# Four pairs of conv gate tiles by seven quarter products in a Hymba-style layer on one Trainium2 core

## The chip, the core and the metric

The kernel runs on one core of a Trainium2 chip. The metric is the device time of one execution in microseconds (us). The core has a matrix engine (TensorE; PE in the profile, PEld for its weight loads), a vector engine (VectorE, DVE), a scalar engine (ScalarE, ACT), GpSimd (POOL), and queues of transfers (DMA) that are issued by SyncE (SP), GpSimd and ScalarE. TensorE writes to PSUM, the other engines work on SBUF and, GpSimd excepted in this kernel, on PSUM.

## The reference

One decoder layer over 1024 tokens of width 1024, all in float32. `w_in` has 5 x 1024 columns; each block of 1024 columns is eight tiles of 128 channels.

```
h = rmsnorm(x, norm_g) * (1.0 + scale) + shift
u = h @ w_in
cv, cg, cs, lx, ls = split(u, 5)
v = cv * sigmoid(cg)
v = causal_depthwise_conv(v, dw_w, dw_b)          # 31 taps
v = silu(layernorm(v, cln_g, cln_b))
y_conv = (v @ pw2_w + pw2_b) * silu(cs)
xs = causal_depthwise_conv(lx, sc_w, sc_b)        # 4 taps
r, i = sigmoid(blockdiag(xs, wr) + br), sigmoid(blockdiag(xs, wi) + bi)
a = exp(-8 * r * softplus(-lam)); bx = sqrt(1 - a*a) * (i * xs)
y_lru = linear_scan(a, bx) * silu(ls)
x = x + (1.0 + gate) * (concat([y_conv, y_lru]) @ w_out)
return rmsnorm(x, final_g)
```

`shift`, `scale` and `gate` come from `silu(c) @ mod_w + mod_b`.

## The kernel before

**Layout.** Channels lie on the 128 partitions, tokens along the free axis (T = 1024, in two halves of H = 512). A product of a tile of 128 output channels is taken in three matmuls for each of the eight input tiles k and each half: the weights are split into a rounded part `whi` and a rest `wlo`, the inputs into `uh` and `ul`, and whi*uh + whi*ul + wlo*uh is summed in PSUM (`mm_k`, L471). A tile is thus 8 x 2 x 3 = 48 matmuls of 128x128 weights against 512 columns. Each weight tile (512 KB) comes by one transfer into one of two `raw` buffers; ScalarE casts it to `whi` (two buffers), VectorE subtracts for `wlo` (two buffers; GpSimd for those whose number is below EARLY = 10).

**Tiles by name.** CV, CG, CS, LX and LS are the tiles of the five blocks of `w_in`. Four of them (FIRST) run while x and the modulation still arrive, three (NEXT: LS 0, CS 0, CS 1) right after, on the not yet normalised input, and are mended afterwards. Then come the other 33 in the order of `slots`, with the block-diagonal gates of an LRU tile between them; then eight LRU tiles of the out projection (`("lru", m)`, inputs `yh`, `yl`), whose results are parked in DRAM; then `pw2`; then the rest of the out projection.

**Seven quarter products.** `pw2` and three pairs of the out projection already use a Strassen-like form (Winograd's) for two output tiles at a time: `pair_weights` forms sums of the quarters of the weights (rows of even and odd k tiles by the two output tiles), `quarters` forms sums of the quarters of the operands (halves of the tokens by even and odd k tiles), and `pair_products` (L593) does seven products of 4 x 3 matmuls each, 84 in place of 96. ScalarE and VectorE join the partial sums (`e`). The names of the operands' quarters are B11 (even tile, first half), B12, B21, B22 (odd tile) and T1 to T4.

**Depthwise conv.** The 31 taps of a conv tile (`conv_tile`) are done in three chains over the even tokens, the odd ones and their sum, each on 512 elements. For five of the eight tiles the chains are 15 + 15 + 14 = 44 VectorE steps (`cacc`, `caccs`) into an accumulator in PSUM, and three half-width folds. For the tiles in POOLED (1, 3, 5) ScalarE makes each product (`cq`, `co`), and GpSimd issues transfers that add it in SBUF to `es` and `oo` (L348, `ADD`): 29 of them for a tile; VectorE does the last three folds. `conv_sum` adds the eight tiles into `csum`, six times on GpSimd and once on VectorE; `layer_norm` starts with its mean on TensorE (L1162).

**LRU.** `gates(i)` runs the two block-diagonal products of tile i, then i*xs on VectorE, `a` and the root on ScalarE, the scan and the product with silu(ls) on VectorE; `split` then makes `yh`, `yl`. **Dots.** The modulation's dot products (`dot`) multiply a tile `modw` with silu(c) and sum along the row, in one VectorE instruction each.

**Order of the work.** No loop fixes the order of the instructions. Each operation is entered in a plan (`S.op`) with an engine, a cost, a priority, and what it reads and writes. `order` (class `Plan`) then goes through simulated time, takes for each free engine the ready operation of lowest priority value that finds its buffers free, and writes the instructions out in that order; on the chip each engine runs its list in that order and waits where something isn't ready. The plan has 47 buffers of 512 KB in SBUF ("big") and three double tiles and two single ones in PSUM. It holds that a VectorE and a GpSimd operation on SBUF exclude each other (`lock`). The priority of an operation of slot n is near n; transfers have values ahead of the work that needs them.

## Time and profile before

| | us |
|---|---|
| median of 3 executions | 742.85 (742.84 to 742.89) |
| the profiled execution, its own time | 742.67 |
| its span, first to last instruction | 740.8 |
| TensorE busy | 728.4 |
| VectorE busy | 633.3 |
| ScalarE busy | 440.6 |
| GpSimd busy | 113.4 |

One execution is profiled; the 1.87 us between its own time and its span lie ahead of the first and behind the last instruction. A row of a view by groups names line, engine, operation, the tile written and the tiles read, the count, the busy time and mean duration in ns of one, and, behind a second bar, the idle time of that engine just before such an instruction with what ended it. A row of the chain of waits or of the timeline begins with its start and its length in us. A row of waits gives the sum, the count and the longest. L343 is the line of a helper through which all elementwise operations with two tensors go, so those are told apart by the names of their tiles.

### The profile page before, as it was taken

Reading aid. Unit: us, or ns where it says so; the run is one execution under the profiler, and the core shown is the slowest. Engines: PE = TensorE matmul, PEld = TensorE weight load, DVE = VectorE, ACT = ScalarE, POOL = GpSimd, SP = SyncE. Lnnn points to the kernel's source line nnn. Section 1 sums busy time; section 2 is a strip of 40 time slices with the busy share of each in tenths; the row PEclk is TensorE's granted clock in tenths of the full one; section 3 lists DMA queues with packets and bytes.
Section 4 is the critical chain, followed back from the end, with each engine's and each line's share of the span. In section 5 each row is a group of like instructions: output and inputs, shape, how many; then the busy total and the mean of one; then the engine's idle time right before and its main releaser. Section 6 shows DMA issues by size and latency. Waiting matters only on the chain.

```text
span 740.8 us, 8887 instructions
## 1 busy us (share of the span) xinstructions
PE 728.4 (98%) x3302; PEld 604.3 (82%) x3302; DVE 633.3 (85%) x847; ACT 440.6 (59%) x544; POOL 113.4 (15%) x115
## 2 busy tenths in 40 slices
PE   9999999999999999999999999999999999999995
PEld 8888887887888888888887888878888888877885
DVE  6999999899999893788499997958799767999845
ACT  7560598558858957846939777634754224455421
POOL 0033021120322233232216110010000000000003
PEclk9999999999999999999999999999999999999997
DMA  9953036673897899999573455425233430623206
GB/s 330 405 177 114 0 98 130 141 145 91 157 217 187 204 231 232 210 240 214 113 156 71 113 113 169 141 87 199 86 113 123 163 113 1 227 88 111 85 1 228
DMA packets 37340, 111.59 MB, mean 151 GB/s; under 512 B 4144, under 2 KB 12848, under 8 KB 37296
## 3 DMA queue, kind: packets, MB, share of 16 engines
q1 hardware_dynamic: 24048, 76.10, 29.2%
q0 software_dynamic: 12528, 34.26, 25.7%
q10 hardware_dynamic: 720, 0.66, 0.3%
q8 instruction: 26, 0.43, 0.2%
q14 instruction: 18, 0.15, 0.1%
HBM read 64.16 MB, written 12.58 MB: 104 GB/s over the span
## 4 chain that ended last, share of the span: by engine, by line
PE 90%; DVE 7%; ACT 2%; issue 1%; POOL 0%; DVEq 0%; POOLq 0%
PE ps L471 65%; PE papw L593 5%; PE first L735 5%; PE pbpw L593 4%; PE pbout L593 2%; PE paout L593 2%; PE gate L1126 2%; PE out L654 1%; DVE fin L335 1%; PE late L735 1%; DVE rawout L343 1%; DVE l34out L343 1%; DVE o L335 1%; DVE yu L343 0%; DVE yt L343 0%
## 5 line engine op out<-in xcount | busy, mean ns | idle before, releaser
L471 PE MATMUL ps<-uh,whi 128*128 128x512 f32 x576 | 177.9, 390 | 0.9 <-ACT sls L324 0.6
L471 PE MATMUL ps<-uh,wlo 128*128 128x512 f32 x576 | 177.4, 389 | 0.0
L471 PE MATMUL ps<-ul,whi 128*128 128x512 f32 x576 | 177.3, 389 | 0.0
L471 PEld LDWEIGHTS ps<-uh,whi 128*128 128x128 f32 x576 | 107.8, 188 | 24.7 <-ACT sls L324 1.5
L471 PEld LDWEIGHTS ps<-uh,wlo 128*128 128x128 f32 x576 | 108.1, 188 | 22.5
L471 PEld LDWEIGHTS ps<-ul,whi 128*128 128x128 f32 x576 | 108.1, 188 | 22.5
L316 ACT CAST whi<-raw 128x1024 fp32r<-128x1024 f32 x46 | 48.1, 1051 | 70.6 <-PE ps L471 59.0
L343 DVE TENSOR_TENSOR wlo<-raw,whi 128x1024 fp32r<-128x1024 f32 x40 | 50.6, 1264 | 16.3 <-ACT whi L316 16.3
L348 POOL DMA_DIRECT2D es<-cq x45 | 39.8, 900 | 134.4 <-ACT cq L324 103.0
L324 ACT ACT_TABLE_LOAD x46 | 59.0, 1283 | 1.5 <-PEq L1428 0.7
L335 DVE SCALAR_TENSOR_TENSOR cacc<-v,V,cacc 128x511 f32<-128x511 f32 (+14 forms) x75 | 55.5, 740 | 0.4
L348 POOL DMA_DIRECT2D oo<-co x42 | 38.8, 968 | 96.5 <-ACT co L324 76.9
L335 DVE SCALAR_TENSOR_TENSOR caccs<-v,V,caccs 128x511 f32<-128x511 f32 (+6 forms) x70 | 52.0, 743 | 1.0
L335 DVE SCALAR_TENSOR_TENSOR caccs<-c,wsum,caccs 128x511 f32<-128x511 f32 (+6 forms) x70 | 52.0, 742 | 0.7
L343 POOL TENSOR_TENSOR o<-fin,bc 128x256 f32<-128x256 f32 (+1 forms) x7 | 6.6, 967 | 245.5 <-ACT bc L316 245.5
L471 PE MATMUL ps<-yh,whi 128*128 128x512 f32 x128 | 40.0, 394 | 0.0
L471 PE MATMUL ps<-yh,wlo 128*128 128x512 f32 x128 | 39.4, 389 | 0.0
L471 PE MATMUL ps<-yl,whi 128*128 128x512 f32 x128 | 39.4, 389 | 0.0
L324 ACT ACTIVATE cq<-v,V 128x511 f32<-128x511 f32 (+14 forms) x45 | 31.6, 706 | 0.0
L335 DVE SCALAR_TENSOR_TENSOR xs<-ps,V,xs 128x1023 f32<-128x1023 f32 (+2 forms) x24 | 30.6, 1275 | 0.4 <-ACT xs L324 0.4
L324 ACT ACTIVATE cq<-c,wsum 128x512 f32<-128x512 f32 x42 | 29.7, 711 | 0.0
L324 ACT ACTIVATE co<-v,V 128x511 f32<-128x511 f32 (+13 forms) x42 | 29.1, 706 | 0.0
(325 smaller groups left out, 1432.5 us busy)
## 6 DMA issues: line engine op xcount, KB each, us to landing
raw<-in_w_in_dram SPq DMA_DIRECT2D x36, 512.0 KB, 4.8
modw<-in_mod_w_dram SPq DMA_DIRECT2D x24, 512.0 KB, 6.3
raw<-in_w_out_dram SPq DMA_DIRECT2D x10, 512.0 KB, 3.9
scsd<-scs SPq DMA_DIRECT2D x8, 512.0 KB, 3.4
acc<-in_xT_dram SPq DMA_DIRECT2D x8, 512.0 KB, 5.4
accd<-acc SPq DMA_DIRECT2D x8, 512.0 KB, 2.8
rawpw<-in_pw_dram SPq DMA_DIRECT2D x8, 512.0 KB, 3.5
scsr<-scsd SPq DMA_DIRECT2D x8, 512.0 KB, 5.3
```

The lines of the kernel that those rows point to most:

```text
L316: act.copy(out(), in_())
L324: act.activation(out=out(), in_=in_(), func=func, **kw)
L335: dve.scalar_tensor_tensor(out=out(), in0=in0(), scalar=scalar, in1=in1(), op0=op0, op1=op1, accum_out=accum)
L343: lambda: e.tensor_tensor(out=out(), in0=a(), in1=b(), op=op), prio, r, w,
L348: return S.op("POOL", ISSUE, lambda: pool.dma_start(out(), a(), accum_op=ALU.add), prio, r, w, lag=RATE * n / T, after=after)
L471: pe.matmul(ps()[:, a - off:b - off], k3(lhs)()[:, k, :], rhs[k]()[:, a:b], start=(k == 0 and lhs is wh and rhs is xh and (a - off) % H == 0),
L593: pe.matmul(half(*ps)(), half(*lhs)()[:, j * P:j * P + P], half(*rhs)(), start=start and j == 0 and z == 0, stop=j == KT // 2 - 1 and z == ...
L654: pe.matmul(ps()[:, a - off:e - off], k3(lhs)()[:, k, :], rhs()[:, i * H + a % H:i * H + a % H + e - a], start=k == KORD[0] and lhs is wh ...
L735: pe.matmul(ps()[:, a - off:b - off], fw_part(lhs, k, i * P, i * P + P)(), rhs()[:, a:b], start=k == 0 and lhs is wh and rhs is xh, stop=k ...
L1126: pe.matmul(ps()[:, c0:c1], lhs()[:, j, :], rhs()[:, c0:c1], start=st == 0, stop=st == 2)
```

## The change

The eight CS tiles are no longer run singly. They become four pairs (PAIRS) of seven quarter products each, behind all other tiles of `w_in` and ahead of the LRU tiles of the out projection, in the order p1, p0, p2, p3.

- Their weights come ordered by even and odd output columns, and `pair_weights` forms their sums, for pairs 0, 2 and 3 on GpSimd and for pair 1 on VectorE (WPAIR).
- The operand sums T1 to T4 of the normalised input are formed early (`h_sums`, four calls t0 to t3 in ORDER) from x, which is put into DRAM after the inputs are made and read back; differences are taken on VectorE, casts on ScalarE, rests on VectorE; the 16 results go to DRAM and come back, by transfers that GpSimd issues, when the pairs are near (`products_of_h`). B11, B21 and B22 are the inputs themselves; the buffers of the even tiles are split in two (`Split`) so that one half can be freed alone.
- `evac_pair` joins the partial sums, takes the SiLU and parks the two tiles in DRAM, as was done with each CS tile before.
- POOLED goes from three conv tiles to two (0 and 3). These keep two accumulators in turn for each chain, and GpSimd does their folds and the last adds.
- `csum` starts as a copy of one tile by a transfer and is added to by six accumulating transfers and one VectorE operation.
- The two gate products of an LRU tile (GTT) and the dots of the gate modulation (GDOT) go from VectorE to GpSimd, the latter with a sum on ScalarE.
- NEXT becomes CG 2, CV 2 and CG 3. The order of all other tiles and gates is written out (ORDER).
- Tiles that wait long (v of three conv tiles, four c, seven y, scan results) are put into DRAM and read back (`spill`, `recall`), with transfers on SP.
- Priorities, reserves and the queues of some last stores are set anew.

The core of the diff:

```diff
-NEXT = (("in", LS), ("in", CS), ("in", CS + 1))
+NEXT = (("in", CG + 2), ("in", CV + 2), ("in", CG + 3))
+PAIRS = tuple((CS + i, CS + i + 1) for i in range(0, KT, 2))
+ORDER = "i24 g0 i25 i33 g1 i32 i3 i26 g2 i35 i34 i12 i4 i36 i27 g3 i28 g4 i37 i13 t0 t1 i5 i29 g5 i30 i38 i39 i31 t2 g7 g6 i14 i6 t3 i15 i7 T p1 p0 p2 p3"
+WPAIR = ('POOL', 'DVE', 'POOL', 'POOL', 'POOL', 'POOL', 'DVE', 'POOL')
+CUTF, TFP = (5, 22)
+TSTEP, TPR = (-30.2, -34.3)
+TENG = ("DVE",) * 4
+FPLAIN = False
+VAWAY = (0, 1, 2, 4, 5)
+VP = 5
+QF = (36.4, 5.4, 32.9, 19.4, 3.9, 13.4, 28.4, 17.4)
+QL = (19.0, 10.0, 17.5, 0.5, 3.0, 22.5, 6.5, 4.0)
+CUT = 3
+HSAWAY = (0, 1, 2, 3, 4, 5, 6)
+HSR = -156.0
-SPARE = 5
+SPARE = 7
-HRES = 4
-POOLED = (1, 3, 5)
+HRES = 2
+POOLED = (0, 3)
-AP = {0: (), 512: (5,), 768: (1, 3, 5, 7)}
+AP = {0: (), 512: (1, 3, 5, 7), 768: (1, 3, 5, 7)}
-SUMS = (0, 1, 3, 2, 6, 4, 7, 5)
+SUMS = (2, 0, 1, 4, 3, 5, 6, 7)
-SPP = 30
+SPP = 25
+CSP, CBP = (-5, 20)
+AWAY = (0, 3, 6, 7)
+YAWAY = (0, 1, 2, 3, 4, 5, 7)
+YOP = 0
+XRT, XSL = "DVE", "DVE"
+GTT = 'POOL'
+WN = 3
+XSP = 6
-GDOT = "DVE"
-FOLD = "DVE"
+GDOT = 'POOL'
+FOLD = 'POOL'
-GM = 22
+GM = 19
...
     slots = list(FIRST + NEXT)
...
+    for x in ORDER.split():
+        i = int(x[1:] or 0)
+        slots.append(("in", i) if x[0] == "i" else ("gate", i) if x[0] == "g" else
+                     ("sums", 0) if x[0] == "T" else ("sums_of", i) if x[0] == "t" else
+                     ("pair", *PAIRS[i]))
     slots += [("lru", m) for m in range(KT)]
-    wslots = [s for s in slots if s[0] != "gate"] + [("out", m) for m in (4, 5, 6, 7)]
-    number = {s: n for n, s in enumerate(wslots)}
+    number = {}
+    for s in slots + [("out", m) for m in (4, 5, 6, 7)]:
+        if s[0] not in ("gate", "sums", "sums_of"):
+            number[s] = sum(1 + (z[0] == "pair") for z in number)
     B0, C0, D0 = 40, 48, 56
 
...
-    def pair_weights(kind, p, n, after, later=(), eng="DVE"):
-        src = [(w_out if kind == "out" else pw2)[2 * p + i] for i in (0, 1)]
-        name = f"{kind}{p}"
+    def pair_weights(kind, p, n, after, later=(), eng="DVE", qf=1.4, ql=2.5):
+        if kind == "in":
+            src = [w_in[m] for m in p]
+            name = f"in{p[0]}"
+        else:
+            src = [(w_out if kind == "out" else pw2)[2 * p + i] for i in (0, 1)]
+            name = f"{kind}{p}"
...
-            DMA(n - 2.5, lambda b=b: b().rearrange("p (k c) -> p k c", k=KT),
+            DMA(n - ql, lambda b=b: b().rearrange("p (k c) -> p k c", k=KT),
                 lambda i=i: src[i][:, :, :], FULL_BYTES, w=[b], after=after)
...
-        q = n - 1.4
+        q = n - qf
...
+    dshift = ctile("dshift", KT // 2)
+
+    def h_sums(j, pr, after):
...
+        d = dshift[:, j:j + 1]
+        S.op("DVE", 0.2, lambda: dve.tensor_tensor(
+            out=d, in0=shift[:, 2 * j + 1:2 * j + 2], in1=shift[:, 2 * j:2 * j + 1],
+            op=ALU.subtract), pr, [("shift", 2 * j), ("shift", 2 * j + 1)], [("dshift", j)],
+            lock=True)
+        x0, x1 = (big_buf(f"xb{2 * j + i}", parts=2) for i in (0, 1))
+        for i, x in enumerate((x0, x1)):
+            recall(pr - 1, ("x", 2 * j + i), x, after)
+
+        def sub(to, a, b):
+            TT(pr, TENG[j], half(*to), half(*a), half(*b), ALU.subtract, H, r=[a, b], w=[to])
+        sub((x0, 0), (x0, 1), (x0, 0))
+        sub((x0, 1), (x1, 1), (x0, 1))
+        sub((x1, 1), (x1, 1), (x0, 0))
+        sub((x1, 0), (x1, 0), (x1, 1))
+        for x, z, b, key in ((x0, "c", d, ("dshift", j)),
+                             (x1, "d", shift[:, 2 * j + 1:2 * j + 2], ("shift", 2 * j + 1))):
+            hi, lo = (big_buf(f"t{z}{a}{j}", F32R, 2) for a in "hl")
+            ACT(pr, half(hi, 0), half(x, 0), "copy", H, r=[(x, 0)], w=[(hi, 0)])
+            SUB(pr, "DVE", half(lo, 0), half(x, 0), half(hi, 0), H, [(x, 0), (hi, 0)],
+                [(lo, 0)])
+            ACT(pr, half(hi, 1), half(x, 1), AF.Identity, H, bias=b, r=[(x, 1), key],
+                w=[(hi, 1)])
+            STT(pr, half(lo, 1), half(x, 1), b, lambda hi=hi: half(hi, 1)().bitcast(F32),
+                ALU.add, ALU.subtract, H, r=[(x, 1), (hi, 1), key], w=[(lo, 1)])
+            for a, t in (("h", hi), ("l", lo)):
+                spill(pr, (f"t{z}{a}", j), t, lambda t=t: t().bitcast(F32))
+
+    def products_of_h(pr, after):
...
+        res = {q: [] for q in ("B11", "B21", "B22", "T1", "T2", "T3", "T4")}
+        for z, qs, late in (("c", ("T1", "T3"), 0), ("d", ("T4", "T2"), TSTEP)):
+            for j in range(KT // 2):
+                hi, lo = (big_buf(f"h{z}{a}{j}", F32R, 2) for a in "hl")
+                for a, t in (("h", hi), ("l", lo)):
+                    m = (f"t{z}{a}", j)
+                    S.op("POOL", ISSUE, lambda t=t, m=m: pool.dma_start(t(), kept[m]),
+                         pr + late, [("kept", m)], [t], after=after, lag=1.5, flight=5.0)
+                for i, q in enumerate(qs):
+                    res[q].append(((hi, i), (lo, i)))
+        for j in range(KT // 2):
+            res["B11"].append(tuple((hh[2 * j].bufs[0], i) for i in (0, 1)))
+            for i, q in enumerate(("B21", "B22")):
+                res[q].append(((hh[2 * j + 1], i), (hl[2 * j + 1], i)))
+        return res
+
 
     def softplus8(pr):
         lam = lambda: V[:, OFF["lam"]:OFF["lam"] + KT]
...
+    sig, kept = {}, {}
+
+    def spill(pr, m, t, src=None):
+        name = "kept%s" % (m if isinstance(m, int) else "%s%d" % m)
+        kept[m] = dram.tile([P, T], F32, tag=name, name=name)
+        DMA(pr, lambda: kept[m], src or t, FULL_BYTES, r=[t], w=[("kept", m)])
+
+    def recall(pr, m, t, after=()):
+        DMA(pr, t, lambda: kept[m], FULL_BYTES, r=[("kept", m)], w=[t], after=after)
+
...
         ci, vi = big_buf(f"c{i}", parts=2), v[i]
+        if i in VAWAY and i not in POOLED and turn:
+            spill(VP - 10, ("v", i), vi)
+            vi = big_buf(f"vb{i}")
+            recall(VP, ("v", i), vi, turn[-1:])
 
 
         b2, src_s = bias2[:, i:i + 1], half(ci, 0)
...
+        es, oo, adds = [big_buf(f"es{i}_{z}", parts=2) for z in "ab"], big_buf(f"oo{i}", parts=2), []
...
+            if r > 1:
+                adds.append(ADD(pr, part(to, r, T), part(q, r, T), r=[to, q], w=[to]))
...
+        ADD(pr, part(oo, 0, H), part(oo, H, T), H, r=[oo], w=[(oo, 0)])
+        ADD(pr, es[0], es[1], r=es, w=[es[0]])
...
         c[i] = ci
 
     def conv_sum():
-        for i in SUMS[1:]:
-            a, eng = (c[SUMS[0]] if i == SUMS[1] else csum), "DVE" if i == SUMS[-1] else "POOL"
-            TT(1000 + 5 * i, eng, csum, a, c[i], ALU.add, r=[a, c[i]], w=[csum])
+        for z, i in enumerate(SUMS):
+            pr, t = 1000 + 5 * i, c[i]
+            if z == 0:
+                DMA(CSP + i, csum, t, FULL_BYTES, r=[t], w=[csum])
+            elif z == KT - 1:
+                TT(pr, "DVE", csum, csum, t, ALU.add, r=[csum, t], w=[csum])
+            else:
+                ADD(pr, csum, t, r=[csum, t], w=[csum])
+            if i in AWAY:
+                spill(CSP + i, ("c", i), t)
+                c[i] = big_buf(f"cb{i}", parts=2)
+                recall(CBP, ("c", i), c[i], [started[CBP]])
+
+
...
+    def evac_pair(ms, ps, e, n, after):
...
+        ts = [big_buf(f"silu{m}", parts=2) for m in ms]
+        for (i, h), (src, key) in ps.items():
+            if h == 2:
+                continue
+            to, k = half(ts[i], h), (ts[i], h)
+            if i or h:
+                TT(pr, "DVE", to, src, half(e, 0), ALU.add, H, r=[key, (e, 0)], w=[k])
+            else:
+                ACT(pr, to, src, AF.Silu, n=H, r=[key], w=[k])
...
+        ACT(pr, half(ts[0], 1), half(ts[0], 1), AF.Silu, n=H, r=[(ts[0], 1)], w=[(ts[0], 1)])
+        ACT(pr, ts[1], ts[1], AF.Silu, r=[ts[1]], w=[ts[1]])
+        for m, t in zip(ms, ts):
+            if m < LS:
+                spill(pr, m, t)
+            else:
+                sls[m - LS] = t
+                lru_out(m - LS, pr + 0.1, after)
+
...
         pr = n + 1.0
-        TT(pr, "DVE", xs, g, xs, ALU.mult, r=[g, xs], w=[xs])
+        TT(pr, GTT, xs, g, xs, ALU.mult, r=[g, xs], w=[xs])
...
-        TT(pr, "DVE", xs, xs, r, ALU.mult, r=[xs, r], w=[xs])
+        TT(pr, XRT, xs, xs, r, ALU.mult, r=[xs, r], w=[xs])
         S.op("DVE", 2.2, lambda: dve.tensor_tensor_scan(
             out=r(), data0=a(), data1=xs(), initial=0.0, op0=ALU.mult, op1=ALU.add),
             pr, [a, xs], [r])
-        t = sls.pop(i)
-        TT(pr, "DVE", t, t, r, ALU.mult, r=[t, r], w=[t])
-        yh[i], yl[i] = big_buf(f"yh{i}", F32R), big_buf(f"yl{i}", F32R)
-        split(B0 - 2 + 0.2 * i, yh[i], yl[i], t, reserve=SPARE)
+        hs[i] = r
+        if i in sls:
+            lru_out(i, pr)
+        elif i in HSAWAY:
+            spill(pr, ("hs", i), r)
+
+    def lru_out(i, pr, after=()):
+        t, r = sls.pop(i), hs.pop(i)
+        if ("hs", i) in kept:
+            r = big_buf(f"hs{i}")
+            recall(pr - HSR, ("hs", i), r, after)
+        TT(pr, GTT, t, t, r, ALU.mult, r=[t, r], w=[t])
+        if i in YAWAY:
+            spill(pr, ("y", i), t)
+        y[i] = t
 
     softplus8(SPP)
-    n, started, acc_d = 3, {}, {}
+    last_pair = [s for s in slots if s[0] == "pair"][-1]
+    n, started, acc_d, paired = 3, {}, {}, False
     for s in slots[4:]:
         if s[0] == "gate":
             gw_load(s[1], n)
             gates(s[1], n + 0.9)
             continue
+        if s[0] == "sums_of":
+            h_sums(s[1], n + TFP, [started[n - CUTF]])
+            continue
+        if s[0] == "sums":
+            h_sets = products_of_h(n + TPR, [started[n - CUT]])
+            continue
+        while len(modt) < 3 * KT and n >= GM + len(modt) - 2 * KT:
+            gate_mod(len(modt) - 2 * KT, n, [started[n - 1]] if n - 1 in started else [])
+        if s[0] == "pair":
+            n += 2
+            w = pair_weights("in", s[1:], n - 1, [started[n - WN]], [started[n - WN + 1]],
+                             WPAIR[PAIRS.index(s[1:])], QF[PAIRS.index(s[1:])],
+                             QL[PAIRS.index(s[1:])])
+            ops, e, ps = next(pair_products(f"in{s[1]}", n - 1, w, h_sets,
+                                            plain=FPLAIN and not paired))
+            started[n - 1], started[n], paired = ops[0], ops[3], True
+            evac_pair(s[1:], ps, e, n, [ops[1]])
+            if s is last_pair:
+                for i in range(KT):
+                    t = y[i]
+                    if i in YAWAY:
+                        t = big_buf(f"yb{i}")
+                        recall(B0 - 2 + 0.2 * i, ("y", i), t, [ops[YOP]])
+                    yh[i], yl[i] = big_buf(f"yh{i}", F32R), big_buf(f"yl{i}", F32R)
+                    split(B0 - 2 + 0.2 * i, yh[i], yl[i], t, reserve=SPARE)
+            continue
         n += 1
         if s not in NEXT:
-            weights(s)
-        if GM <= n < GM + 8:
-            gate_mod(n - GM, n, [started[n - 2]] if n - 2 in started else [])
+            weights(s, [started[n - 3]] if paired else [])
         m = s[1]
         ps = mm_tile(f"ps{n}")
         if n == len(FIRST + NEXT):
             inputs()
+            for k in range(KT):
+                spill(XSP, ("x", k), xt[k])
         xh, xl = {"in": (hh, hl), "lru": (yh, yl)}[s[0]]
         if s in NEXT:
...
+    for m in sum(PAIRS, ()):
+        w_in[m] = by_parity(w_in[m:m + 1])[0]
     w_first = w_in[[m for _, m in FIRST]].transpose(1, 2, 0, 3).reshape(P, KT, -1)
     w_out = g["w_out"][0]
     arrays = {
```

120 lines of the change are left out of this document (69 added, 51 removed).

## The prediction

> **What bounds the kernel now.** I read the page first, then the busy time by stages, then the chain of waits, then TensorE's own waits.
>
> ```profile
> span 740.8 us, 8887 instructions
> PE 728.4 (98%) x3302; PEld 604.3 (82%) x3302; DVE 633.3 (85%) x847; ACT 440.6 (59%) x544; POOL 113.4 (15%) x115
> ...
> GB/s 330 405 177 114 0 98 130 141 145 91 157 217 187 204 231 232 210 240 214 113 156 71 113 113 169 141 87 199 86 113 123 163 113 1 227 88 111 85 1 228
> DMA packets 37340, 111.59 MB, mean 151 GB/s; under 512 B 4144, under 2 KB 12848, under 8 KB 37296
> ...
> q0 software_dynamic: 12528, 34.26, 25.7%
> ```
>
> TensorE is busy for 98% of the span, VectorE (DVE) for 85%. The busy time by stages says where the rest lies; the columns are PE, PEld, DVE, ACT, POOL, granted clock, DMA share and GB/s. The second row ends at the mean of the layer norm, the fourth at the first pw2 product.
>
> ```profile
> 0.00:58.70 58.70, 57.19 (x288) 48.71 (x289) 52.86 (x108) 37.17 (x54) 9.44 (x10) 1.00 0.77 288
> 58.70:491.20 432.50, 431.57 (x1907) 356.38 (x1906) 376.01 (x480) 295.56 (x356) 97.41 (x99) 1.00 0.65 151
> 491.20:522.40 31.20, 31.20 (x151) 25.71 (x151) 22.08 (x20) 13.32 (x13) 0.00 (x0) 1.00 0.41 149
> 522.40:568.70 46.30, 46.30 (x205) 38.32 (x205) 46.26 (x56) 28.90 (x33) 0.00 (x0) 1.00 0.28 95
> 568.70:634.70 66.00, 66.00 (x293) 54.62 (x292) 50.53 (x65) 23.05 (x28) 0.00 (x0) 1.00 0.35 122
> ```
>
> From 58.7 to 634.7 us TensorE has no gap worth naming (0.93 us in all) at full clock: every matmul taken out there is worth its own time, as long as nothing else becomes late. VectorE is the next limit: up to the first pw2 product it is busy 52.86 + 376.01 + 22.08 + 46.26 = 497.2 of 568.7 us, and all of that (the depthwise conv, its sum, the layer norm, the operands of pw2) has to be done before pw2 can run.
>
> **The change, part by part.** First the products. The chain of waits gives the price of both forms:
>
> ```profile
> 233.23 54.40 PE ps L471 x240
> ...
> 568.67 5.44 PE papw L593 x24
> 574.12 5.44 PE pbpw L593 x24
> 579.55 5.44 PE papw L593 x24
> 585.00 2.72 PE pbpw L593 x12
> 587.72 5.44 PE papw L593 x24
> ```
>
> A plain matmul costs 54.40 / 240 = 0.2267 us, and two plain tiles are 96 of them: 21.76 us. A pair by seven products is 84, and pw2's first pair runs from 568.67 to 587.72: 19.05 us. Four pairs save 4 x 2.71 = 10.8 us; by count, 48 x 0.2267 = 10.88 us, which I take. All other TensorE work is the same in amount.
>
> Next VectorE, which pays for it. The prices:
>
> ```profile
> L343 DVE TENSOR_TENSOR wlo<-raw,whi 128x1024 fp32r<-128x1024 f32 x40 | 50.6, 1264 | 16.3 <-ACT whi L316 16.3
> L335 DVE SCALAR_TENSOR_TENSOR cacc<-v,V,cacc 128x511 f32<-128x511 f32 (+14 forms) x75 | 55.5, 740 | 0.4
> L335 DVE SCALAR_TENSOR_TENSOR caccs<-v,V,caccs 128x511 f32<-128x511 f32 (+6 forms) x70 | 52.0, 743 | 1.0
> L335 DVE SCALAR_TENSOR_TENSOR modw<-modw,sc 128x1024 f32<-128x1024 f32 x23 | 27.8, 1217 | 0.0
> L343 DVE TENSOR_TENSOR rawpw<-rawpw,rawpw 128x512 f32<-128x512 f32 x12 | 8.2, 687 | 0.2
> L343 DVE TENSOR_TENSOR epw<-epw,pbpw 128x1024 f32<-128x1024 f32 x4 | 4.9, 1220 | 5.0 <-PE pbpw L593 5.0
> L343 DVE TENSOR_TENSOR sls<-sls,r 128x1024 f32<-128x1024 f32 x8 | 9.8, 1220 | 0.1
> ```
>
> - One more conv tile on VectorE: 44 steps x 0.74 = 32.6, and three folds x 0.687 = 2.1. The nine folds of the pooled tiles go to GpSimd: -6.2. Together +28.5.
> - Sums of the operands (h_sums): for each of four j six half-width operations x 0.687 and two x 0.74: 5.6; +22.4.
> - Evacuating a pair: one full-width add, 1.22, and three half-width, 2.06; four times: +13.1.
> - Weights: eight single splits x 1.264 go, -10.1; the one pair on VectorE costs three full and five half operations, 3.66 + 3.43 = +7.1.
> - Gate products to GpSimd: two for each of eight tiles x 1.22, -19.5. The eight gate dots to GpSimd, x 1.217: -9.7.
>
> Sum: 28.5 + 22.4 + 13.1 - 10.1 + 7.1 - 19.5 - 9.7 = +31.8 us on VectorE, all due before the first pw2 product. ScalarE loses 47 products of a conv tile and gets some casts and eight accumulations, and stays far from full. The wait that this adds to VectorE's own queue is that for GpSimd, next.
>
> What goes to GpSimd: three pairs of weights (three full and five half operations, 5.5 full ones, each), 16 gate products, eight dots, six half folds: 16.5 + 16 + 8 + 3 = 43.5 full-size operations; six sums of csum go (they become transfers): +37.5. At the row's 2.4 us they are 90 us on an engine that is busy 113 of 741 us, so GpSimd has room. But the two engines are not independent:
>
> ```profile
> 291.63 2.39 POOL L343 TENSOR_TENSOR csum<-c,c 128x1024 f32<-128x1024 f32 x1 [8.32 <-DVE c L343]
> 392.37 2.38 POOL L343 TENSOR_TENSOR csum<-csum,c 128x1024 f32<-128x1024 f32 x1 [8.35 <-DVE c L343]
> 395.30 2.79 POOL L343 TENSOR_TENSOR csum<-csum,c 128x1024 f32<-128x1024 f32 x1
> 400.37 3.25 POOL L343 TENSOR_TENSOR csum<-csum,c 128x1024 f32<-128x1024 f32 x1 [2.27 <-DVE c L343]
> 404.18 2.68 POOL L343 TENSOR_TENSOR csum<-csum,c 128x1024 f32<-128x1024 f32 x1
> ...
> 392.76 3.07 DVE L343 TENSOR_TENSOR wlo<-raw,whi 128x1024 fp32r<-128x1024 f32 x1
> 397.05 1.33 DVE L343 TENSOR_TENSOR glo<-graw,ghi 128x256 fp32r<-128x256 f32 x1
> 401.28 4.63 DVE L335 SCALAR_TENSOR_TENSOR cacc<-v,V,cacc 128x504 f32<-128x504 f32 x6
> 405.82 2.14 DVE L335 SCALAR_TENSOR_TENSOR r<-a,r 128x1024 f32<-128x1024 f32 x1
> ...
> 293.76 1.35 DVE L343 TENSOR_TENSOR xs<-g,xs 128x1024 f32<-128x1024 f32 x1 [2.31 <-ACT g L324]
> ```
>
> Each time an operation with two inputs in SBUF waits until GpSimd's is over: wlo takes 3.07 against 1.26 in its mean row, and r and glo lose some 0.9 each; the conv steps, whose accumulator is in PSUM, run on beside GpSimd (six in 4.63). The four sums from 392 to 407 us cost VectorE 1.85 + 0.92 + 0 + 0.92 = 3.7 us, the one at 291.63 some 0.1 (xs at 293.76), and the sixth, at 481, met an idle VectorE: 3.8 / 6 = 0.64 us for an operation. The bounds for the new ones are 0 (each beside conv steps) and 1.85 (each meets such an operation at once). I take 0.64, as the new operations too stand beside a conv stage that is half PSUM steps: 37.5 x 0.64 = 24.0 us. The Trainium skill, "SBUF — State Buffer", section Who interferes with whom, has the same split (two SBUF inputs against a GpSimd operation that reads SBUF) and says that the loser blocks for the whole instruction; if every one of the 37.5 blocked VectorE for the 2.4 us of its row, that would be 90 us in place of 24. The rows here agree with the kind of operation and show the wait to be partial on average.
>
> Now the sum for the stage up to pw2. Need: 497.2 + 31.8 + 24.0 = 553.0 us of VectorE. Room: the stage shrinks to 568.7 - 10.9 = 557.8 us, and idle time that I hold to be lost in any case is 5.8 us of the start and 9.1 us of the layer norm's round trip (rows 1 and 3 of the stages): 542.9 us. It lacks 10.1 us. The next stage has 66.0 - 50.53 = 15.5 us of idle VectorE, and the operands of the later pw2 products can slip into it; I let 5 us slip (nothing to all 10.1), and TensorE waits for the other 5.1.
>
> Transfers: x out and back 16, operand sums 32, v of three tiles 6, c of four 8, y of seven 14, scan results of two 4: 80 x 512 KB = 42 MB more; one conv tile less takes some 11 MB off GpSimd's queue and csum puts 4 back. 112 becomes about 146 MB, 200 GB/s in the mean, where the page's slices reach 240 in the conv stage without a gap on TensorE. I cost them at nothing; what covers them is the double buffer of the weights, whose loads land in 4.8 us of an 11 us tile. Without it, see the third rival.
>
> The rest I cost at nothing: the three early tiles change from an LRU gate and two conv gates to inputs of the conv, with as many operations; the pooled conv keeps two accumulators in turn, with 29 accumulating transfers to a tile as before; three more of the last stores go over ScalarE's queue, and the tail keeps its length. What would be late if this cover went is named in the rivals.
>
> Forecast: 742.67 (the profiled execution's own time; 1.87 us lie around its span) - 10.88 + 5.1 = 736.9, and 0.18 more for the median: **737.0 us**.
>
> **Rivals.**
>
> 1. VectorE fits. If GpSimd's operations fall beside PSUM steps (0.3 us each, 11 us), the need is 540 of 542.9 and nothing is lost: 742.85 - 10.88 = 732.0 us. For it: row 400.37 met no wait at all. Against: three of the four neighbours did.
> 2. The port gives it back. At L us of wait per operation, TensorE waits 497.2 + 31.8 + 37.5 L - 542.9 - 5 = 37.5 L - 18.9 us; from L = 0.79 on the change is slower. At L = 1.0 it is 742.85 - 10.88 + 18.6 = 750.6; at 1.85, 782. For it: 0.79 is close to my 0.64, and weights and gate products meet splits, which have two SBUF inputs. Against: most VectorE time added is conv steps in PSUM. The Trainium skill, "Perfetto Trace Analysis", section Optimizing Scalar/DVE Operations, warns of this: moving work between these two engines might not help, since they share a port.
> 3. GpSimd's queue. It now holds transfers that bring the operand sums back, gate products on which the recurrence waits, and adds that wait for ScalarE, in one order:
>
> ```profile
> POOL es L348 <- ACT cq L324: 103.0, 22, 15.2
> ...
> raw<-in_w_in_dram SPq DMA_DIRECT2D x36, 512.0 KB, 4.8
> ...
> PE ps L471 <- ACT sls L324: 0.6, 2, 0.3
> PE ps L471 <- ACT sig L324: 0.3, 1, 0.3
> ```
>
> The longest wait in it is 15.2 us. A load of an operand sum, or the weight sums of a pair, behind such a wait stops TensorE for up to that, once: 742.85 - 10.88 + 15.2 = 747.2. The SP queue has the like with its 64 more transfers. For it: 22 such waits. Against: none reached TensorE, whose own waits between the start and pw2 are the two of 0.6 and 0.3 us.
> 4. It doesn't do what it says: TensorE's instructions must fall by 48; were there none fewer, 742.85 or more. The code leaves no room for it.
>
> **How the numbers follow.** About 0.2% (1.5 us) is what a measurement here can tell from no change. Chances: the forecast 0.40 (0.36 faster, 0.03 same, 0.01 slower), rival 1 0.20 (all faster), rival 2 0.24 (0.02, 0.02, 0.20), rival 3 0.16 (0.02, 0.01, 0.13), rival 4 nil. Faster 0.60, same 0.06, slower 0.34. The range: its low end is rival 1 with half a microsecond to spare, 731.5; the high end takes in rival 3 and rival 2 up to about L = 1.05, 753; some 0.12 is left above. The forecast's own range is 732 to 742 (slip of all 10.1 us, or of none).
>
> **What would show it.** TensorE 48 matmuls and about 10.9 us less; four pairs at 19.05 us each. VectorE busy before pw2 at about 550 us and hardly idle; splits of 2 to 3 us beside GpSimd operations; the mean of the layer norm at about 485 and the first pw2 product at about 563. If the mean stands where it did or earlier and TensorE is full, rival 1 holds. If TensorE waits for VectorE for 15 us or more, rival 2; if it waits for loads or for GpSimd's sums, rival 3. The forecast is wrong if the idle time of TensorE before pw2 is below 2 or above 10 us more than now.

## The result and the profile after

The changed kernel takes 767.87 us (median of 4 runs, 766.50 to 768.85) against 742.85: the ratio is 1.0338, with a 95% interval of 1.032 to 1.0356. The forecast was 737.0 with a range up to 753, so the sign was wrong and the time lies outside the range. The profiled run took 767.88 us.

The page of the changed kernel, its lines that answer to those of before (the DMA row is the mean busy share of the 16 DMA engines in 40 slices of 19.2 us, in tenths; before, a slice is 18.5 us):

```profile
span 766.1 us, 9079 instructions
PE 725.9 (95%) x3254; PEld 599.1 (78%) x3254; DVE 672.7 (88%) x905; ACT 437.7 (57%) x545; POOL 200.6 (26%) x159
...
PE   9999999999998399959999999999999999999995
...
DMA  9945354498999972995998443976412451523206
...
q1 hardware_dynamic: 32976, 109.79, 39.4%
q0 software_dynamic: 11520, 34.38, 21.9%
```

The two rows of the page of before that the prediction did not show:

```profile
DMA  9953036673897899999573455425233430623206
...
q1 hardware_dynamic: 24048, 76.10, 29.2%
```

TensorE has its 48 matmuls less (3254 against 3302) and yet ends 25.3 us later. The page gives the split. At the rate of before, the matmuls would take 728.4 - 10.9 = 717.5 us; they took 725.9, so 8.4 us went to slower matmuls. TensorE was idle for 766.1 - 725.9 = 40.2 us against 740.8 - 728.4 = 12.4, so 27.8 us went to new waits: 27.8 + 8.4 - 10.9 = 25.3.

The busy time by stages of the changed kernel says where (PE, PEld, DVE, ACT, POOL, granted clock, DMA share, GB/s; the first two rows end at the mean of the layer norm and at the first pw2 product):

```profile
58.70:524.20 465.50, 437.10 (x1898) 357.50 (x1896) 416.92 (x538) 293.72 (x358) 185.46 (x143) 0.97 0.74 214
524.20:593.80 69.60, 69.60 (x320) 57.52 (x320) 64.93 (x71) 40.47 (x44) 0.00 (x0) 1.00 0.37 126
...
190.00:265.00 75.00, 58.95 (x252) 47.03 (x251) 53.42 (x67) 44.20 (x63) 25.30 (x24) 0.90 1.01 275
...
320.00:346.00 26.00, 17.61 (x68) 13.43 (x67) 14.47 (x16) 14.88 (x20) 11.05 (x8) 0.87 1.05 311
```

The same two stretches of the kernel before:

```profile
190.00:265.00 75.00, 75.00 (x332) 62.15 (x331) 69.67 (x88) 57.02 (x76) 22.02 (x26) 1.00 0.94 206
...
320.00:346.00 26.00, 26.00 (x116) 21.54 (x115) 23.52 (x34) 14.04 (x18) 8.40 (x10) 1.00 1.06 224
```

From 58.7 us to the mean TensorE loses 465.5 - 437.1 = 28.4 us, 24.4 of them in two stretches (16.05 in 190 to 265, 8.39 in 320 to 346). There VectorE is not full either: 53.42 of 75 and 14.47 of 26 us. What is full is the DMA share, 1.01 and 1.05. But before, the share in the same stretches was 0.94 and 1.06, and TensorE had no gap. So a full share alone can't be the reading; what hangs on the transfers, or how long the line of them is, must have changed.

The chain of waits of the changed kernel names transfers; before, none stood in the same view. Four of its five rows of transfers (the fifth is a load of weights, 3.8 us):

```profile
203.70 11.38 DMA xb<-keptx
...
218.83 16.04 DMA keptv<-v
234.96 9.58 DMA vb<-keptv
...
320.53 18.66 DMA xb<-keptx
```

These four are transfers that the change added: x read back for the operand sums (`h_sums`), and one conv tile put into DRAM and read back (`spill`, `recall`). Together they are 55.7 us of the chain. The transfers by line of the changed kernel, with the median us from issue to landing in the last column:

```profile
raw<-in_w_in_dram SPq DMA_DIRECT2D x28, 512.0 KB, 4.9
modw<-in_mod_w_dram SPq DMA_DIRECT2D x24, 512.0 KB, 9.2
...
xb<-keptx SPq DMA_DIRECT2D x8, 512.0 KB, 13.5
...
kepttdh<-tdh SPq DMA_DIRECT2D x4, 512.0 KB, 16.3
...
vb<-keptv SPq DMA_DIRECT2D x3, 512.0 KB, 9.6
```

Over the whole run the weights' median hardly moved (4.8 to 4.9 us), which is the row that the prediction leaned on. In the crowded stretch from 190 to 265 us it did, here after and then before:

```profile
raw<-in_w_in_dram SPq DMA_DIRECT2D x5, 512.0 KB, 9.2
```

```profile
raw<-in_w_in_dram SPq DMA_DIRECT2D x6, 512.0 KB, 5.0
```

Still, no wait of the changed kernel ends with such a load. The plan orders every list as if what SyncE loads were there 5 us behind its issue (LANDING) or sooner. Of the new transfers, x and v read back and the writes of the operand sums take 9.6 to 16.3 us in the median; those in quieter stretches take less (the writes of x, c and y 2.8 to 3.1).

How one late transfer becomes several stops is to be read in the timeline of the changed kernel from 239 to 263 us, by engine (start, length, engine and line, what it does; in brackets the idle time of that engine just before, and what ended it):

```profile
239.63 1.25 SPq L400 DMA_DIRECT2D modw<-in_mod_w_dram  x1
...
244.62 0.78 ACT L362 ACTIVATE cacc<-vb,V 128x512 f32<-128x512 f32 x1 [8.03 <-DMA vb<-keptv]
...
245.94 1.03 ACT L354 CAST whi<-raw 128x1024 fp32r<-128x1024 f32 x1
...
256.62 1.06 ACT L362 ACTIVATE modw<-modw 128x1024 f32<-128x1024 f32 x1 [8.54 <-POOL modw L381]
...
261.32 1.03 ACT L354 CAST xsh<-xs 128x1024 fp32r<-128x1024 f32 x1
...
254.24 2.34 POOL L381 TENSOR_TENSOR modw<-modw,sc 128x1024 f32<-128x1024 f32 x1 [13.41 <-DMA modw<-in_mod_w_dram]
...
244.66 0.69 DVE L381 TENSOR_TENSOR c<-vb 128x512 f32<-128x512 f32 x1 [6.96 <-DMA vb<-keptv]
...
251.53 1.22 DVE L381 TENSOR_TENSOR wlo<-raw,whi 128x1024 fp32r<-128x1024 f32 x1
...
252.81 0.79 PE L504 MATMUL ps<-ua,wlo 128*128 128x512 f32 x1 [4.57 <-DVE wlo L381]
...
262.40 1.22 PE L1286 MATMUL gate<-xsh,ghi 128*128 128x512 f32 x2 [8.38 <-ACT xsh L354]
```

SyncE, ScalarE, GpSimd and VectorE each work through a written order. By the chain above, the load of `vb` can't be issued before the write `keptv` has landed (218.83 + 16.04), so it stands at 234.96 and lands at 244.5. ScalarE waits 8.03 us for it, and the cast of the weights (`whi`, 245.94) stands behind that wait although its own data, issued at 219.96, had landed at 237.7. VectorE waits for it too, does its conv steps first, and `wlo` comes at 251.53: TensorE stops for 4.57 us. Meanwhile a tile of modulation weights, issued at 239.63, reaches GpSimd at 254.24, 14.6 us later. GpSimd has stood for 13.41 us, ScalarE's sum of that product stands behind GpSimd for 8.54, and the cast `xsh`, which the next gate needs, stands behind the sum and six products of the conv: TensorE stops for 8.38 us more. (The input of `xsh` was itself late, ready at 257.6, since VectorE had come late to it.) That GpSimd does these products, with a sum on ScalarE, is itself part of the change (GDOT).

### The profile page after: what moved, and what is told of

Its sections match the earlier page's. It is cut to its first block, busy times and chain, and to the rows that moved or that the text cites. A ratio compares the mean times of both kernels' runs of the same rounds, so it can differ in the third digit from the quotient of the medians.

```text
span 766.1 us, 9079 instructions
## 1 busy us (share of the span) xinstructions
PE 725.9 (95%) x3254; PEld 599.1 (78%) x3254; DVE 672.7 (88%) x905; ACT 437.7 (57%) x545; POOL 200.6 (26%) x159
## 2 busy tenths in 40 slices
DMA packets 45693, 145.79 MB, mean 190 GB/s; under 512 B 5072, under 2 KB 11728, under 8 KB 45648
## 3 DMA queue, kind: packets, MB, share of 16 engines
q1 hardware_dynamic: 32976, 109.79, 39.4%
q10 hardware_dynamic: 1152, 1.05, 0.4%
## 4 chain that ended last, share of the span: by engine, by line
PE 62%; DVE 16%; DMA 8%; issue 6%; ACT 4%; POOL 4%; SPq 0%; DVEq 0%; POOLq 0%; ACTq 0%
PE ps L504 33%; PE papw L634 5%; PE first L777 5%; DMA xb<-keptx 4%; PE pbpw L634 4%; PE pain L634 2%; PE pbout L634 2%; PE paout L634 2%; PE pbin L634 2%; DMA keptv<-v 2%; PE gate L1286 2%; DVE wlo L381 2%; DVE caccs L373 2%; PE out L696 1%; DVE r L1298 1%
## 5 line engine op out<-in xcount | busy, mean ns | idle before, releaser
L504 PE MATMUL ps<-ua,whi 128*128 128x512 f32 x224 | 88.5, 395 | 4.6 <-ACT whi L354 2.0
L504 PE MATMUL ps<-ub,whi 128*128 128x512 f32 x224 | 87.7, 392 | 0.0
L504 PE MATMUL ps<-ul,whi 128*128 128x512 f32 x224 | 69.4, 391 | 0.0
L504 PE MATMUL ps<-uh,whi 128*128 128x512 f32 x224 | 69.4, 391 | 0.0
L504 PE MATMUL ps<-uh,wlo 128*128 128x512 f32 x224 | 69.4, 391 | 0.0
L504 PEld LDWEIGHTS ps<-ul,whi 128*128 128x128 f32 x224 | 42.3, 189 | 8.9
L504 PEld LDWEIGHTS ps<-uh,wlo 128*128 128x128 f32 x224 | 42.3, 189 | 8.8
L504 PEld LDWEIGHTS ps<-uh,whi 128*128 128x128 f32 x224 | 42.3, 189 | 8.8
L504 PE MATMUL ps<-ua,wlo 128*128 128x512 f32 x112 | 44.1, 393 | 4.6 <-DVE wlo L381 4.6
L504 PE MATMUL ps<-ub,wlo 128*128 128x512 f32 x112 | 43.8, 391 | 0.0
L504 PE MATMUL ps<-yl,whi 128*128 128x512 f32 x128 | 39.5, 390 | 0.0
L504 PE MATMUL ps<-yh,wlo 128*128 128x512 f32 x128 | 39.4, 389 | 0.0
```

Of the source, the lines that this page charges most:

```text
L504: pe.matmul(ps()[:, a - off:b - off], k3(lhs)()[:, k, :], rhs[k]()[:, a:b], start=(k == 0 and lhs is wh and rhs is xh and (a - off) % H == 0),
```

## The experiments

All kernels of the study beside the two, with the profiled run's span and TensorE's busy time, idle = span - busy, and slower = busy - 717.5 (for the kernel before with more writes, busy - 728.4):

| kernel | us | span | TensorE busy | idle | slower |
|---|---|---|---|---|---|
| before | 742.85 | 740.8 | 728.4 | 12.4 | |
| after | 767.87 | 766.1 | 725.9 | 40.2 | 8.4 |
| e1_no_spills | 743.96 | 742.2 | 719.9 | 22.3 | 2.4 |
| e2_small_pool | 757.62 | 755.9 | 721.7 | 34.2 | 4.2 |
| e3_v_stays | 765.70 | 763.9 | 723.6 | 40.3 | 6.1 |
| e4_sums_stay | 750.47 | 748.7 | 723.1 | 25.6 | 5.6 |
| e5_both | 738.24 | 736.3 | 719.1 | 17.2 | 1.6 |
| e6_new_plan | 755.70 | 753.9 | 724.6 | 29.3 | 7.1 |
| e7_new_plan2 | 759.56 | 758.3 | 726.0 | 32.3 | 8.5 |
| e8_before_more | 746.76 | 745.0 | 730.6 | 14.4 | 2.2 |
| e9_new_plan3 | 749.91 | 746.5 | 720.9 | 25.6 | 3.4 |
| e10_new_plan4 | 746.53 | 744.6 | 720.8 | 23.8 | 3.3 |
| e11_small_spills | 749.62 | 747.8 | 721.0 | 26.8 | 3.5 |
| e12_unbound_spills | 761.28 | 759.2 | 725.6 | 33.6 | 8.1 |

Kernels 1 to 5, 8, 11 and 12 have one run each, beside a kernel before of 742.8 to 743.1; 6, 7 and 9 have four, 10 has six. The changed kernel's own four lie between 766.50 and 768.85, so 1 or 2 us between single runs say little. Theory A was that the added transfers cost the time, theory B that GpSimd's work does (the port and its slow products).

**Without the writes (e1).** The order of all instructions stays; the added writes into DRAM are left out and the read-backs take rows of x. The expectations count 38 of these writes; the list of transfers has 40 (8 of x, 16 of operand sums, 7 of y, 4 of c, 3 of v, 2 scan results), and the bytes agree: 145.79 - 124.81 = 21.0 MB, 40 times 512 KB.

```diff
     def spill(pr, m, t, src=None):
         name = "kept%s" % (m if isinstance(m, int) else "%s%d" % m)
-        kept[m] = dram.tile([P, T], F32, tag=name, name=name)
-        DMA(pr, lambda: kept[m], src or t, FULL_BYTES, r=[t], w=[("kept", m)])
+        if isinstance(m, int):
+            kept[m] = dram.tile([P, T], F32, tag=name, name=name)
+            DMA(pr, lambda: kept[m], src or t, FULL_BYTES, r=[t], w=[("kept", m)])
+            return
+        kept[m] = xT[m[1] * P:m[1] * P + P, :]
+        S.op("SP", max(0.1, FULL_BYTES / 360e3), lambda: None, pr, [t], [("kept", m)])
```

> The order of the instructions on every engine is that of the changed kernel. The 38 transfers that put x, the operand sums, v, c, y and scan results into DRAM are left out (the eight parked gate tiles stay), and those that bring them back read rows of x in their place, so 20 MB less is moved and no read-back waits for a write; the output is not the reference's. Theory A (in the crowded stretches transfers land in 10 to 19 us where the plan counts on 5, and ScalarE and GpSimd, which take their work in order, hold the weights' casts behind what waits for them): most of the 28 us of TensorE's idle time and of the 7 us of lowered clock goes, 738 to 750 us. Theory B (VectorE loses its time to GpSimd at their common port, as forecast): the port sees the same work, 762 to 768 us.

It took 743.96 us, 23.9 less than the changed kernel, within the range of theory A. The 40 read-backs stay, so what they cost is not in this. In its profile the stage and the landings read:

```profile
190.00:265.00 75.00, 71.89 (x314) 58.23 (x313) 67.97 (x87) 58.77 (x78) 31.70 (x29) 1.00 1.01 246
...
320.00:346.00 26.00, 26.00 (x116) 21.55 (x115) 25.89 (x31) 21.93 (x28) 14.68 (x10) 1.00 0.40 93
```

```profile
vb<-in_xT_dram SPq DMA_DIRECT2D x3, 512.0 KB, 4.2
```

The DMA share in 190 to 265 is still 1.01, with TensorE at 71.89 of 75 us. So the share alone is a poor gauge: it says that the engines were never idle, not how long the line in front of them was. The landings say that: `vb` 4.2 in the median in place of 9.6.

**GpSimd's work cut to an eighth (e2).** Its elementwise operations act on an eighth of their width, or fill their output with zeros where it is a new tile.

```diff
     def TT(prio, eng, out, a, b, op, n=T, r=(), w=(), reserve=0, after=()):
         e = dve if eng == "DVE" else pool
+        if eng == "POOL" and prio < D0 + 20:
+            same = set(S.keys(w)) <= set(S.keys(r))
+            w8 = lambda f: (lambda: f()[..., :f().shape[-1] // 8])
+            if same:
+                out, a, b = w8(out), w8(a), w8(b)
+            else:
+                return S.op(eng, p_cost(n), lambda: pool.memset(out().bitcast(F32), 0.0), prio,
+                            r, w, reserve=reserve, lock=not in_psum(r), after=after)
```

> Same order; all transfers stay. GpSimd's elementwise operations ahead of the last stage do an eighth of their columns where they work in place, and a fill with zeros that reads nothing where they write a new tile (the rests of weight splits); the output is not the reference's. Theory B: the wait at the port goes and the sums come sooner, 740 to 750 us. Theory A: TensorE's stops at 244 to 265 and 320 to 346 us stay, since loads still land late; some 2 to 6 us for the splits that ran late, 760 to 767 us.

757.62 us, 10.2 less, which lies between the ranges of the two theories. Its page and its waits on TensorE:

```profile
PE 721.7 (95%) x3254; PEld 596.6 (79%) x3254; DVE 652.9 (86%) x905; ACT 436.9 (58%) x545; POOL 115.8 (15%) x159
```

```profile
PE gate L1294 <- ACT xsh L354: 8.3, 1, 8.3
PE ps L512 <- DVE wlo L389: 4.6, 1, 4.6
```

VectorE's busy time falls by 672.7 - 652.9 = 19.8 us. Its 905 operations are the same, so this is what waiting beside GpSimd had cost it. But the two stops of 8.4 and 4.6 us remain at their size: the port did not make them.

**Both (e5).**

> Order of the changed kernel on every engine, with what e1 leaves out (38 transfers into DRAM) and what e2 leaves out (seven eighths of GpSimd's elementwise work, fills in place of rests); the output is not the reference's. Theory A plus B (late transfers cost 24 us and GpSimd's operations 10 us, and together they are the whole loss): they add up to 767.9 - 24 - 10 = 734, that is 732 to 737 us, the 10.9 us of the products in full. If they share one cause (either of them alone would free the same wait), 740 to 744 us. If a third cause is left, above 737 without GpSimd or transfers in TensorE's waits.

738.24 us, 29.6 less; the two alone would sum to 34.1, so they overlap by 4.5, and a third cause is left, as the last case of the expectation has it. TensorE's longest wait is 1.5 us. It is 4.6 us below the kernel before. Of the 6.3 us that part it from 742.85 - 10.88 = 731.97, the table shows 4.8 as idle time over that of before and 1.6 as slower matmuls, in small pieces that were not followed further.

**Which writes (e3, e4).** e3 leaves out only the three writes of v, e4 only the sixteen of the operand sums.

Both diffs in one; each kernel has its own condition, and the lines behind it are the same:

```diff
+        if isinstance(m, tuple) and m[0] == "v":        # e3
+        if isinstance(m, tuple) and m[0][0] == "t":     # e4
+            kept[m] = xT[m[1] * P:m[1] * P + P, :]
+            S.op("SP", max(0.1, FULL_BYTES / 360e3), lambda: None, pr, [t], [("kept", m)])
+            return
```

> Same order; only the three transfers that put v of conv tiles 2, 4 and 5 into DRAM are left out, and their read-backs read rows of x; the output is not the reference's. SyncE no longer holds its queue for the landing of one (13.0 us at 222 to 235 us). If that one round trip is what is late (ScalarE waits 8.0 us for it with a cast of weights behind it), 8 to 13 us are won: 755 to 760 us. If the stretch as a whole is too full (theory A with the gate dots' loads, the x read-backs and the weights late as well), 0 to 6 us: 762 to 768 us. Theory B: 767 us.

> Same order; only the 16 transfers that put the operand sums into DRAM are left out (8.4 MB of the 14 or so MB that the two crowded stretches move beyond what they moved before), and their read-backs read rows of x; the output is not the reference's. Theory A by fullness: 10 to 20 us are won, 748 to 758 us. If the round trip of v alone counts: 0 to 5 us, 763 to 768 us. Theory B: 767 us.

e3: 765.70 us, 2.2 less, hardly more than the changed kernel's own spread; the idle time is unchanged. The round trip of `v` stands in the chain with 25.6 us, and taking its write away gave 2.2 at most: what ends a wait last is not what the wait is worth. That the next late transfer is right behind is the likely reason, not shown by itself. e4: 750.47, 17.4 less, within the range of theory A by fullness. The operand sums carry most of it, though not one of them stands in the chain.

**Bytes or SyncE's queue (e11, e12).** A write does two things: it moves 512 KB, and it holds SyncE's list until its data are there. e11 keeps the second (the 40 writes wait as before, but move 32 of 1024 columns), e12 the first (full writes, which never wait, since they come from rows of x in DRAM; so they go from DRAM to DRAM, where the changed kernel's go from SBUF, and SyncE's queue takes 39.5% of the engines' time against 39.4%). In both the read-backs take rows of x. The two diffs against e1 in one, rewritten to stand together (`e12` in the place of `e11`):

```diff
-        S.op("SP", max(0.1, FULL_BYTES / 360e3), lambda: None, pr, [t], [("kept", m)])
+        w = dram.tile([P, T], F32, tag=name, name=name)
+        e11 = lambda: sp.dma_start(w[:, :32], (src or t)()[:, :32])
+        e12 = lambda: sp.dma_start(w, xT[m[1] * P:m[1] * P + P, :])
+        S.op("SP", max(0.1, FULL_BYTES / 360e3), e11, pr, [t], [("kept", m)])
```

> Same order as the changed kernel; the 38 writes into DRAM stay in SyncE's queue and wait for their data as before, but each writes only 32 of 1024 columns, and the read-backs read rows of x (so the values are not the reference's). Leaving the writes out altogether gave 743.96 us against 767.87. Theory 1 (the bytes crowd the DMA engines and make the other transfers late): the time is that of the kernel without the writes, 743 to 748 us. Theory 2 (SyncE's queue is held by writes whose data are late, and the loads behind them are issued late; the bytes themselves do little): it stays at 760 to 768 us. If both count, between, and the distance from 744 is SyncE's share.

> The counterpart: same order; each of the 38 writes still moves 512 KB into DRAM, but from rows of x in DRAM, so that it never waits for data; the read-backs read rows of x (values not the reference's). Theory 1 (the bytes): 758 to 768 us, since the engines are as full as in the changed kernel. Theory 2 (SyncE's queue held): 743 to 750 us. If the two shares add, the losses against 743.96 of this kernel and of the one with small writes sum to about 24 us.

e11: 749.62, which is 5.7 us over e1. e12: 761.28, which is 17.3 over e1. So both count, and the shares add up to 23.0 of 23.9. That a read-back waits for its write to land is in neither; the 0.9 us left for it are no more than the spread of the runs. The stage of 190 to 265 us in e11, and then in e12:

```profile
190.00:265.00 75.00, 72.25 (x315) 58.58 (x314) 70.00 (x86) 58.90 (x80) 31.58 (x29) 1.00 1.02 244
```

```profile
190.00:265.00 75.00, 64.40 (x272) 51.47 (x272) 59.50 (x72) 48.74 (x67) 25.87 (x25) 0.93 1.03 285
```

The gap comes back with the bytes (64.40 of 75 us busy, against 58.95 in the changed kernel) and stays nearly closed without them. So about three quarters of the loss are the bytes on full DMA engines, and about one quarter is SyncE's list.

**The same crowding on the kernel before (e8).** 24 writes of 512 KB (12.6 MB) are added to the kernel before, each behind a weight load, with the order unchanged.

```diff
-        DMA(p_load, cut(rw), lambda: wsrc(s)[:, c, :], n * P * 4, w=keys(rw), after=first_load)
+        def load():
+            sp.dma_start(cut(rw)(), wsrc(s)[:, c, :])
+            z = number[s]
+            if 10 <= z < 34:
+                more = dram.tile([P, T], F32, tag=f"more{z}", name=f"more{z}")
+                sp.dma_start(more, uhs[z % KT]().bitcast(F32))
+        S.op("SP", n * P * 4 / 360e3, load, p_load, (), keys(rw), after=first_load)
```

> The kernel before, its order unchanged, with 24 transfers of 512 KB (12.6 MB) more: behind the load of each weight tile from number 10 to 33 SyncE also writes a resident operand tile to DRAM, which nobody reads. If full DMA engines alone stop TensorE (theory A in its strong form), the kernel before, which has stages with all of them busy too, slows by 8 us or more: 751 us or more. If the changed kernel's order is what can't take late landings (nothing in the kernel before waits for a transfer that has just been written, and no ScalarE work ahead of a cast waits for one), 743 to 747 us.

746.76 us, 3.9 more than the 742.85 of before, for 12.6 MB, within the range of the second case. The 40 writes of e12 are 21.0 MB and cost 17.3. That is 0.31 against 0.82 us per MB: the old order takes crowding better than the new one. The places differ, so this is a hint at the order and no proof.

**Other orders for the same work (e6, e7, e9, e10).** The plan was given one line for all transfers, served in order of issue, and holds a tile as ready, and its buffer as free, only when that line has served it; then its constants were chosen again (the order of the tiles, which tiles go to DRAM, the engine for the dots, priorities). Of the diff of e10:

```diff
+            late = 0.0
+            if o.lag or o.eng == "SP":
+                self.wire = max(self.wire, end - o.cost) + (o.lag * WSUM if o.lag else o.cost) * WIRE
+                late = self.wire + WLAT
...
-            o.end = end
+            o.end = max(end, late)
...
-                    heapq.heappush(releases, (end, b.name, b.pool))
+                    heapq.heappush(releases, (max(end, late), b.name, b.pool))
...
-GDOT = 'POOL'
+GDOT = 'DVE'
+WIRE, WLAT, WSUM = 1.03, 2.5, 0.83
```

> All of the changed kernel's computation, in an order planned anew: the plan now counts the transfers of all queues against one server (1.5 us for 512 KB, 2.9 us for an accumulating one), holds a buffer until its transfer has landed, and the constants (order of the tiles, what is parked in DRAM, priorities) are chosen under it; dots back on VectorE, v of other tiles and two c in place of four parked. Theory A (the old plan gave transfers 5 us wherever they stood): with landings in the plan most of the stops go, 732 to 742 us. If the work itself is too much for VectorE and the transfers, whatever the order: 745 us or more.

> A second order planned anew in the same way, another set of constants: v is never parked, folds on VectorE, the operand sums spread over the stage with one of the four early. Theory A: 731 to 742 us. If the work itself is too much: 745 us or more.

> All of the changed kernel's computation in a third new order. The plan counts transfers as in the first two; its constants were chosen by replaying the finished order with three settings of the transfers' times (up to 3.5 us for an accumulating one) and with the clock that falls after an idle stretch, against which the first two were not tested. Theory A: an order that takes late landings gets most of the products' 10.9 us: 734 to 745 us. If the work is too much in any order: 750 us or more, like the first two.

> A fourth new order, chosen in the same way, with another set of parked tiles and one of the operand sums early. Theory A: 732 to 745 us. If the work is too much in any order: 750 us or more.

755.70 (ratio to before 1.0173, interval 1.0156 to 1.019), 759.56 (1.0221, 1.0204 to 1.0239), 749.91 (1.0105, 1.0084 to 1.0127) and 746.53 (1.0051, 1.0035 to 1.0068). All four lie above the range of theory A, and none beats the kernel before. The first two lie in the range given for work that is too much in any order, the last two between the ranges, so that rival stands. The last is 21.3 us better than the changed kernel with 48 matmuls fewer than before and nearly as many bytes (140.55 MB against 145.79). What is left in it, from its waits and from ScalarE's timeline:

```profile
PE ps L509 <- ACT sls L367: 6.2, 1, 6.2
```

```profile
276.47 0.62 ACT L359 CAST tch<-xb 128x512 fp32r<-128x512 f32 x1 [10.96 <-DMA oo<-co]
```

It is the same kind of stop: ScalarE stands for 10.96 us behind an accumulating transfer that has not landed. Whether an order exists in which the 10.9 us of the products come through whole, or whether the work is too much in any order, is open.

## Why the prediction was wrong

- **The products: right.** 48 matmuls fewer. A pair of CS tiles takes 84 products in 492.95 - 473.91 = 19.04 us (from the third group of one pair to the third of the next), against 19.05 forecast; the chain of the changed kernel:

```profile
473.91 5.44 PE pain L634 x24
...
492.95 5.44 PE pain L634 x24
```

- **VectorE: right in kind, too dear in size, and not what decided.** Up to pw2 it is busy 52.24 (the start, to 58.7 us) + 416.92 + 64.93 = 534.1 us; 553.0 was the need. Over the whole run it grows by 39.4 us (633.3 to 672.7) against 31.8 + 24.0 = 55.8. The port's part was at most 19.8 us by e2, against 24.0: e2 also cuts what GpSimd does in the kernel before, and no run shows what that had cost there. The own work was thus at least 19.6, against 31.8. A small cause is in the timeline: a conv step shows 0.74 us, and the sum took it so; but steps that take the two chains in turn start every 0.65 us, and only steps of one chain, four of them in 3.09, every 0.77:

```profile
245.27 3.09 DVE L373 SCALAR_TENSOR_TENSOR caccs<-vb,V,caccs 128x505 f32<-128x505 f32 x4
...
248.92 0.74 DVE L373 SCALAR_TENSOR_TENSOR caccs<-vb,V,caccs 128x501 f32<-128x501 f32 x1
249.57 0.75 DVE L373 SCALAR_TENSOR_TENSOR cacc<-vb,V,cacc 128x510 f32<-128x510 f32 x1
```

  The rest was not taken apart. The Trainium skill, "SBUF — State Buffer", section Summary: rules for kernel authors, says that where a VectorE operation with two SBUF inputs meets a GpSimd operation that reads SBUF, the second to issue blocks until the first is done; had each of the 37.5 cost VectorE its full 2.4 us, that would have been an estimated 90 us. e2 shows at most 19.8 for all of GpSimd's operations, so the kind of conflict agrees; how often two of them met was not counted.
- **The forecast's own bottleneck: wrong.** It let TensorE wait 5.1 us for a full VectorE. VectorE was idle for 593.8 - 534.1 = 59.7 us before pw2, so it was not full, and TensorE was idle for 29.9. Rivals 1 and 2 rest on the same balance and fall with it; rival 2 in particular, since e2 gives back only 10.2 us and leaves the large stops. Once the writes are gone, GpSimd's work costs 743.96 - 738.24 = 5.7 us. That this is near the 5.1 is luck as far as the runs show, since VectorE is not full in e1 either (busy for 534.8 us of the 569.8 before pw2).
- **The step that failed: "I cost them at nothing"**, of the 42 MB of transfers. The argument was that slices of 240 GB/s passed without a gap and that the weights' loads land in 4.8 us. Both were true of the kernel before. But GB/s was read as room, when the busy share of the engines in the two stretches of before stood at 0.94 and 1.06: little was left. And the double buffer covers weight loads alone. Those grew to 9.2 us in the crowded stretch and still end no wait; the late transfers of the chain have no such cover, and work that needs nothing of them stands behind their readers in an engine's written order. By e1 the 40 writes, half of the transfers, cost 23.9 us, by e11 and e12 about 17 of that by their bytes and about 6 through SyncE's list. What the other half, the read-backs, cost was not measured.
- **Rival 3 was the right kind, with the wrong price.** It named GpSimd's queue and SP's, and priced one wait of 15.2 us. What came were stops of 8.4, 6.9, 4.6 and several of 1 to 2 us, through ScalarE's and VectorE's order as much as GpSimd's, and 8.4 us of slower matmuls, most of them after these stops, which nothing in the prediction counted. "None reached TensorE" was evidence about the old order only.
- **The signs.** The mean stands at 524.2 (forecast 485), the first pw2 product at 593.8 (563), TensorE's idle time before pw2 grew by 27.5 us (2 to 10 allowed): each of them said that the forecast failed. The sign of rival 3, as written, was TensorE waiting for loads or for GpSimd's sums. It did not come in that form: TensorE's long waits end with ScalarE and VectorE, and the late loads stand steps behind them. TensorE's longest waits in the changed kernel:

```profile
PE gate L1286 <- ACT xsh L354: 9.3, 2, 8.4
PE gate L1286 <- ACT r L362: 6.9, 1, 6.9
PE ps L504 <- DVE wlo L381: 4.6, 1, 4.6
PE ps L504 <- ACT whi L354: 2.0, 1, 2.0
```

## What to carry to other kernels

Read the room for more transfers in the busy share of the DMA engines, stage by stage, and in the longest landing, not in GB/s: stages at 0.94 and 1.06 moved only 206 and 224 GB/s, and had little room. The share alone doesn't say how little: at the same 1.01, from 190 to 265 us, TensorE lost 16.1 us in the changed kernel and 3.1 in e1. For every transfer that a change adds, ask what stands behind its first reader in that engine's order; a late load can hold up all of them, not just the reader. And where a written order rests on an assumed landing time, a change that fills the DMA engines should be planned with the landing times that it makes itself, and even then measured: four orders planned so took 8 to 21 us less than the changed kernel, and none less than the kernel before.
